# Layer 0's queries and keys: from TensorE transposes to VectorE block transposes and a scratch in DRAM

## The chip, the cores and the metric

The kernel runs on one core of a Trainium2 chip. The metric is the device time of one execution in microseconds (us). A measurement of this kernel can tell about 0.2% (4.2 us) from no change. The core has five engines that matter here: TensorE (PE in the profile), VectorE (DVE), ScalarE (ACT), GpSimd (POOL) and SyncE (SP), which issues nearly all of the transfers. Each works through its own instructions in order and waits on semaphores for the others. Weights come from DRAM (HBM) by 16 DMA engines.

## The reference, cut to what matters

Two decoder layers over 256 tokens of width 2048, float32. Layer 0 mixes tokens with block-sparse attention (16 heads of 128; with 256 tokens there is one block, so it is causal attention), layer 1 with latent attention; each is followed by a gated MLP of width 5632. For layer 0:

```python
h = rms_norm(x, attn_norm[0])
q = rope(rms_norm((h @ wq).reshape(B, S, H, dh), gq), pos, rot)   # H = 16, dh = 128, rot = 32
k = rope(rms_norm((h @ wk).reshape(B, S, H, dh), gk), pos, rot)
v = (h @ wv).reshape(B, S, H, dh)
s = einsum('bqhd,bhkd->bhqk', q, k) * dh ** -0.5                   # causal mask, softmax, times v
y = o.reshape(B, S, H * dh) @ wo
```

A product of queries and keys sums over the head's 128 features. TensorE sums over partitions, so queries and keys have to lie with features on partitions, while `h @ wq` and its norm leave them with tokens on partitions. Something has to turn them.

## The kernel before, in words

All products with weights are done in three parts, for accuracy: a float32 weight piece of 128x512 (`raw`) is split into a rounded part (`whi`, cast by ScalarE, L125) and the rest (`wlo`, subtracted by VectorE, L126), activations likewise, and high x high, high x low and low x high are added up in PSUM.

The work is a list of **quanta**, one for each weight piece. In layer 0 a quantum is six matmuls 128x512 (`tok_major`, L262). The 16 heads are handled in four groups of four heads. A group is 48 quanta: 16 for its queries, 16 for its keys, 16 for its values. I number a group's quanta 0 to 47 below; 48 is then the next group's quantum 0. A step f that was put down by `at(q, f)` is written into the program right behind quantum q's matmuls (what was put down by `first_in` stands ahead of it), and this fixes each engine's order. `ws.split` at quantum q casts the piece of quantum q + 3; five buffers of parts let ScalarE and VectorE run up to about two quanta ahead of TensorE. Loads of 1 MB (four pieces, L90) are issued by SP in the same order, each once VectorE is done with the load three before it.

For a group's queries or keys the class `Heads` has these steps, each a method: `evac` (ScalarE, PSUM to SBUF tile `qk`, times the token's norm, L405), `squares` (VectorE, sums of squares, L410), `rstd` (VectorE, then GpSimd's power, L434), `scaled` (VectorE, four instructions of 128x128 for each half of the tokens, L447), `rotate` (VectorE, four small ones, L472 to L478), and `turned` (L487: TensorE transposes of 128x128 against the identity, into PSUM). `queries_out` and `keys_out` then copy from PSUM to the tiles that the scores use: a rounded part and a float32 copy by ScalarE (L630), the rest by VectorE (L637).

`Head.plan(q, q_values)` puts down a head's scores (TensorE) and mask (VectorE) at q, exponentials at q + 1, normalization at q + 2, the turn of the probabilities at q + 6 and the product with the values at `q_values`. In groups 1 to 3 the queries' `evac` stands at quantum 15, the keys' at 31, the values' (`evac_parts`) at 47. In group 0 the queries' stands at 30 and the keys' at 40, since the norm has to be summed first.

Of the kernel before, what the change touches and what calls it, by code (L numbers as in the profile page):

```python
# [17 lines left out]
P = 128  # L18
# [118 lines left out]
def trunk(ctx: ExitStack, tc: tile.TileContext, a, out):  # L137
# [6 lines left out]
    ps_acc = ctx.enter_context(tc.tile_pool(name="ps_acc", bufs=4, space=PSUM))  # L144
    ps_tp = ctx.enter_context(tc.tile_pool(name="ps_tp", bufs=2, space=PSUM))
    ps_sc = ctx.enter_context(tc.tile_pool(name="ps_sc", bufs=2, space=PSUM))
    ctx.enter_context(tc.manual_schedule())

    mm = nc.tensor.matmul
# [231 lines left out]
        nc.sync.dma_start(out[:, j, :], xT[:, j, :])  # L381


    class Heads:


# [65 lines left out]
        def rotate(self, t, stages=range(4)):  # L452
            if not self.rot:
                return
            n, rot = self.n, self.rot
            hf = rot // 2
            tb, C, Sn = self.tabs
            ct = tb[:, C + t * rot : C + (t + 1) * rot]
            st = tb[:, Sn + t * rot : Sn + (t + 1) * rot]
            x = self.x[:, t]  # L460
            def over(s):
                return s[:, None, :].to_broadcast([P, n, s.shape[1]])

            def part(name):
                r = att_pool.tile([P, 16 * 32], F32, name=name, bufs=2)
                return r[:, : n * rot].rearrange("p (n r) -> p n r", n=n)

            if 0 in stages:
                self.rot_parts = part("ro1"), part("ro2")
            t1, t2 = self.rot_parts  # L470
            if 0 in stages:
                nc.vector.tensor_tensor(t1, x[:, :, :rot], over(ct), op=ALU.mult)  # L472
            if 1 in stages:
                nc.vector.tensor_tensor(t2[:, :, :hf], x[:, :, hf:rot], over(st[:, :hf]), op=ALU.mult)
            if 2 in stages:
                nc.vector.tensor_tensor(t2[:, :, hf:], x[:, :, :hf], over(st[:, hf:]), op=ALU.mult)
            if 3 in stages:
                nc.vector.tensor_tensor(x[:, :, :rot], t1, t2, op=ALU.add)  # L478

        def turned(self, dst, pair, i0):  # L480

# [170 lines left out]
    def keys_out(dst, tp, i0, gain=None):  # L652
# [5 lines left out]
        copied(k0[i0 // 2], src[:, :, :P], gain)  # L658
        rest_of(lo, src, hi, gain)

    def evac_parts(state, key, scale):
        v0, v1 = env[key]
        hi, lo = v0[:, 0], v0[:, 1]
        first_, second = (state["acc"][t][:, :512] for t in range(NT))
        if scale is None:
            nc.scalar.copy(hi, first_)
            nc.vector.tensor_tensor(lo, first_, hi.bitcast(F32), op=ALU.subtract)
            nc.scalar.copy(v1, second)
            return
        r = scale()  # L670
        nc.scalar.activation(hi, first_, AF.Copy, scale=r[:, 0:1])
        nc.vector.scalar_tensor_tensor(
            lo, first_, r[:, 0:1], hi.bitcast(F32), op0=ALU.mult, op1=ALU.subtract
        )
        nc.scalar.activation(v1, second, AF.Copy, scale=r[:, 1:2])

    def plan_heads(q, hs, key, out):

        at(q, hs.evac)
        for t in range(NT):  # L680
            at(q + 1 + t, hs.squares, t)
        at(q + 3, hs.rstd)
        for t in range(NT):
            at(q + 6 + 2 * t, hs.scaled, t)
            at(q + 7 + 2 * t, hs.rotate, t)
        for i0 in (0, 2):
            pair = {}
            q1 = q + 11
            at(q1, lambda hs=hs, p=pair, i0=i0: hs.turned(None, p, i0))
            at(q1, lambda p=pair, i0=i0, key=key: out(env[key], p["tp"], i0))  # L690

    at(-1, n1.scaled, 0)
    def signed_gains():
# [11 lines left out]
    for g in range(4):  # L705
        for kind in "qkv":
            state = {"first": g == 0 and kind == "q"}
            for kt in range(KD):
                q = add(tok_major, state, lambda: n1.h, kt, KD - 1)
                if g == 0 and kind == "q" and kt + 1 < KD:  # L710
                    first(q + 1, n1.scaled, kt + 1)
                if g == 0 and kind == "k" and kt < 12:
                    for j in range(kt * 4 // 3, (kt + 1) * 4 // 3):
                        at(q, n1.square, j)
                        at(q + 1, n1.total, j)
            if g == 0 and kind == "q":
                at(q + 14, n1.sums)
            if kind == "q":
                at(q, moba_tiles, g)
            if kind == "v":  # L720
                at(q, evac_parts, state, ("v", g), lambda: n1.rstd)
                q_v = q
            else:
                hs = Heads(state, 4, P, G_Q if kind == "q" else G_K, 32, (tab, T_MC, T_MS), lambda: n1.rstd)
                plan_heads(q + (0 if g else 15 if kind == "q" else 9), hs, ("qT" if kind == "q" else "kT", g),
                           queries_out if kind == "q" else keys_out)
                q_k = q
        for i in range(4):
            hd = Head(
# [2 lines left out]
            )  # L732
            if g < 3:

                q0 = q_k + (14 if g else 22) + i // 2 * 6
                hd.plan(q0, q0 + 12)
            else:
                q0 = q_k + 14 + 2 * i
                hd.plan(q0, max(q0 + 8, q_v + 3 + i))


# [578 lines left out]
```

## Time and profile before

| what | value |
|---|---|
| median of 3 runs | 2083.99 us (2083.98 to 2084.32) |
| span of the profiled execution | 2081.8 us |
| TensorE clock granted | 1.000 |
| VectorE, ScalarE busy | 68%, 55% of the span |
| DMA | 391.82 MB, mean 188 GB/s |
| layer 0's transposes of queries and keys (L487) | 64, starting between 64.6 and 287.0 us |

The profiled execution gives a span of 2081.8 us, from its first instruction to its last; the runs' times include some 2.2 us around it. In a timeline row the first number is the start in us from the span's start, the second how long the row's instructions took from the first's start to the last's end; then engine, line, operation, tiles, shape and count, and in brackets the engine's idle time before it and what ended it. Consecutive instructions overlap a little: an instruction's result is there later than its successor starts, so a row of three instructions of 0.69 us that takes 1.89 us means one every 0.60 us.

### The profile page before, as it was taken

To read this page: it belongs to the slowest core of one execution; us is meant where nothing else is said; L and a number is where in the kernel's file an instruction comes from. 1 tells how busy PE (TensorE), PEld (TensorE's weight loads), DVE (VectorE), ACT (ScalarE), POOL (GpSimd) and SP (SyncE) were. 2 spreads that over 40 slices of the span, in tenths; PEclk is the share of its full clock that TensorE was granted. 3 is DMA by queue.
4 is the path that set the end of the run, shared out by engine and by line. 5 is a ranking of instruction groups with operands and counts; after the bars stand their busy time and mean duration, and the time that the engine had idled before them with its cause. 6 is when DMAs were issued, how large, how long until landed. Compare 5 with 4: busy or idle time off the path is not lost.

```text
span 2081.8 us, 42114 instructions
## 1 busy us (share of the span) xinstructions
PE 2076.9 (100%) x16742; PEld 2011.4 (97%) x16742; DVE 1415.0 (68%) x2915; ACT 1148.0 (55%) x2248; POOL 46.1 (2%) x36
## 2 busy tenths in 40 slices
PE   9999999999999999999999999999999999999999
PEld 7888889999999999999999889999999999999999
DVE  6877676776666766655556898766667666755554
ACT  6555555555555555555455786655555555544443
POOL 0000000000000000000000110000000000000000
PEclk9999999999999999999999999999999999999999
DMA  7445445555555555555554533555555555555553
GB/s 271 174 173 180 166 162 203 183 193 192 200 187 201 186 199 193 193 202 184 201 194 159 203 124 123 195 190 196 190 202 186 200 189 196 196 198 207 198 205 132
DMA packets 59269, 391.82 MB, mean 188 GB/s; under 512 B 6832, under 2 KB 9520, under 8 KB 13248
## 3 DMA queue, kind: packets, MB, share of 16 engines
q1 hardware_dynamic: 58896, 388.83, 51.7%
q8 instruction: 131, 2.15, 0.4%
q14 instruction: 66, 0.54, 0.1%
q10 hardware_dynamic: 144, 0.26, 0.0%
q0 software_dynamic: 32, 0.04, 0.0%
HBM read 387.01 MB, written 2.10 MB: 187 GB/s over the span
## 4 chain that ended last, share of the span: by engine, by line
PE 100%; DMA 0%; issue 0%; ACT 0%; DVE 0%; POOLq 0%
PE acc L288 26%; PE acc L290 26%; PE acc L289 26%; PE acc L262 18%; PE tp L487 1%; PE tp L566 1%; PE sc L495 0%; PE sc L496 0%; PE sc L494 0%; PE sc L584 0%; PE sc L516 0%; DMA par<-in_par 0%; PE sc L532 0%; PE sc L530 0%; PE tp L357 0%; PE sc L527 0%
## 5 line engine op out<-in xcount | busy, mean ns | idle before, releaser
L126 DVE TENSOR_TENSOR wlo<-raw,whi 128x512 fp32r<-128x512 f32 (+1 forms) x1464 | 996.9, 689 | 375.5 <-ACT whi L125 373.6
L125 ACT CAST whi<-raw 128x512 fp32r<-128x512 f32 (+1 forms) x1463 | 871.2, 620 | 466.9 <-PE acc L289 213.1
L288 PE MATMUL acc<-h,whi 128*128 128x256 f32 x2880 | 795.4, 276 | 0.0
L290 PE MATMUL acc<-h,wlo 128*128 128x256 f32 x2880 | 795.0, 276 | 0.0
L289 PE MATMUL acc<-h,whi 128*128 128x256 f32 x2880 | 794.9, 276 | 0.0
L289 PEld LDWEIGHTS acc<-h,whi 128*128 128x128 f32 x2880 | 540.7, 188 | 0.0
L288 PEld LDWEIGHTS acc<-h,whi 128*128 128x128 f32 x2880 | 540.6, 188 | 0.0
L290 PEld LDWEIGHTS acc<-h,wlo 128*128 128x128 f32 x2880 | 540.6, 188 | 0.0
L288 PE MATMUL acc<-a,whi 128*128 128x256 f32 x1408 | 388.6, 276 | 0.0
L290 PE MATMUL acc<-a,wlo 128*128 128x256 f32 x1408 | 388.6, 276 | 0.0
L289 PE MATMUL acc<-a,whi 128*128 128x256 f32 x1408 | 388.6, 276 | 0.0
L262 PE MATMUL acc<-whi,h 128*128 128x512 f32 (+1 forms) x896 | 268.1, 378 | 0.4 <-ACT h L310 0.4
L289 PEld LDWEIGHTS acc<-a,whi 128*128 128x128 f32 x1408 | 264.3, 188 | 0.0
L290 PEld LDWEIGHTS acc<-a,wlo 128*128 128x128 f32 x1408 | 264.3, 188 | 0.0
L288 PEld LDWEIGHTS acc<-a,whi 128*128 128x128 f32 x1408 | 264.3, 188 | 0.0
L262 PEld LDWEIGHTS acc<-whi,h 128*128 128x128 f32 x896 | 164.8, 188 | 30.3 <-ACT h L310 0.9
L262 PE MATMUL acc<-wlo,h 128*128 128x512 f32 (+1 forms) x448 | 168.4, 376 | 0.0
L288 PE MATMUL acc<-oT,whi 128*128 128x256 f32 x512 | 142.7, 279 | 0.0
L290 PE MATMUL acc<-oT,wlo 128*128 128x256 f32 x512 | 141.6, 277 | 0.0
L289 PE MATMUL acc<-oT,whi 128*128 128x256 f32 x512 | 141.5, 276 | 0.0
L808 DVE TENSOR_TENSOR g<-acc,rstd_b 128x256 f32<-128x256 f32 x88 | 37.5, 426 | 126.0 <-PE acc L290 123.1
L815 ACT ACTIVATE c<-g,par 128x256 f32<-128x256 f32 x88 | 53.1, 603 | 108.0 <-DVE g L808 108.0
(190 smaller groups left out, 1633.7 us busy)
## 6 DMA issues: line engine op xcount, KB each, us to landing
raw<-in_ffn_gu SPq DMA_DIRECT2D x176, 1024.0 KB, 4.8
raw<-in_ffn_down SPq DMA_DIRECT2D x88, 1024.0 KB, 4.8
raw<-in_moba_wk SPq DMA_DIRECT2D x16, 1024.0 KB, 4.8
raw<-in_moba_wv SPq DMA_DIRECT2D x16, 1024.0 KB, 4.8
raw<-in_moba_wo SPq DMA_DIRECT2D x16, 1024.0 KB, 4.8
raw<-in_mla_wo SPq DMA_DIRECT2D x16, 1024.0 KB, 4.8
raw<-in_moba_wq SPq DMA_DIRECT2D x12, 1024.0 KB, 4.8
raw<-in_mla_wkv_a SPq DMA_DIRECT2D x8, 576.0 KB, 3.6
```

Source lines behind the costliest of these rows:

```text
L125: self.nc.scalar.copy(hi[:, :n], w)
L126: self.nc.vector.tensor_tensor(lo[:, :n], w, hi[:, :n].bitcast(F32), op=ALU.subtract)
L262: mm(state["acc"][t][:, :n], src[:, kt, c : c + P], (t_lo if part == 1 else t_hi)[:, :n], start=kt == 0 and part == 0, stop=kt == k_last a ...
L288: mm(o, w_hi, src[:, kt, :S], start=first and k == 0, stop=False, skip_group_check=True)
L289: mm(o, w_hi, src[:, kt, S:], start=False, stop=False, skip_group_check=True)
L290: mm(o, w_lo, src[:, kt, :S], start=False, stop=kt == k_last, skip_group_check=True)
L487: nc.tensor.transpose(tp[:, (i * NT + t) * P : (i * NT + t + 1) * P], flat[:, t, c : c + P], ident)
L566: nc.tensor.transpose(tp[:, c * P : (c + 1) * P], self.s[:, c * P : (c + 1) * P], ident)
L808: nc.vector.tensor_tensor(self.g[:, 2:], self.gate["acc"][:, :S], self.norm.rstd_b, op=ALU.mult)
L815: nc.scalar.activation(self.c, self.g[:, 2:], AF.Identity, bias=par[:, cb : cb + 1], scale=self.cw(2))
```

## The change

Queries and keys of layer 0 are no longer turned on TensorE. VectorE transposes 32x32 blocks (`STREAM_TRANSPOSE`, two instructions a tensor, one for each half of the tokens) from `qk` into a tile `blk`. SP writes `blk` to a scratch in DRAM with four transfers, one for each 32 partitions (128 KB each, in runs of 1 KB), and reads it back into `qk` with one transfer (512 KB, 4 KB to a partition), so that block rows land on the partitions of their block column: that completes the transpose. The copies into the scores' tiles now read `qk` in SBUF and not PSUM; for queries there is one of each kind over all four heads where there were two over two heads each.

The schedule moves with it: `scaled` and `rotate` one quantum earlier (5 to 8 after the `evac`, before 6 to 9), the block transposes and the four writes 9 after it, the read back 11 after it, the copies into the scores' tiles 16 after it (before 11, with the transposes). Scores of the heads, and all that follows them, move by four quanta in groups 1 to 3 and by five in group 0.

```diff
+    dram = ctx.enter_context(tc.tile_pool(name="dram", bufs=2, space=bass.MemoryType.DRAM))
+    def cross_out(srcs, b):
+        w = b.shape[1] // P
+        there = dram.tile([4, 32, 4, w * 32], F32, name=f"there{w}")
+        to = b.rearrange("p (j n t c) -> p t n j c", j=4, t=len(srcs), c=32)
+        for t, src in enumerate(srcs):
+            nc.vector.transpose(to[:, t], src.rearrange("p (n j c) -> p n j c", j=4, c=32))
+        for i in range(4):
+            nc.sync.dma_start(
+                there.rearrange("j a i m -> i a j m")[i],
+                b[32 * i : 32 * (i + 1)].rearrange("a (j m) -> a j m", j=4),
+            )
+        return there
+    def cross_in(dst, there):
+        nc.sync.dma_start(dst, there.rearrange("j a i m -> (j a) (i m)"))
...
+        def cross(self):
+            b = att_pool.tile([P, NT * 4 * P], F32, name="blk", bufs=1)
+            self.there = cross_out([self.x[:, t].rearrange("p n d -> p (n d)") for t in range(NT)], b)
+        def crossed(self):
+            cross_in(self.x.rearrange("p t n d -> p (t n d)"), self.there)
...
+    def crossed_queries(dst, hs):
+        q0, q1 = dst
+        src = hs.heads_of().rearrange("p (n t) i c -> p t n i c", t=NT)
+        hi, lo = (q1[:, part].rearrange("p n (i c) -> p n i c", c=32) for part in range(2))
+        nc.scalar.copy(hi, src[:, 1])
+        nc.vector.tensor_tensor(lo, src[:, 1], hi.bitcast(F32), op=ALU.subtract)
+        nc.scalar.copy(q0.rearrange("p n (i c) -> p n i c", c=32), src[:, 0])
...
         for t in range(NT):
-            at(q + 6 + 2 * t, hs.scaled, t)
-            at(q + 7 + 2 * t, hs.rotate, t)
-        for i0 in (0, 2):
-            pair = {}
-            q1 = q + 11
-            at(q1, lambda hs=hs, p=pair, i0=i0: hs.turned(None, p, i0))
-            at(q1, lambda p=pair, i0=i0, key=key: out(env[key], p["tp"], i0))
+            at(q + 5 + 2 * t, hs.scaled, t)
+            at(q + 6 + 2 * t, hs.rotate, t)
+        at(q + 9, hs.cross)
+        at(q + 11, hs.crossed)
+        at(q + 16, lambda: out(env[key], hs))
...
-                q0 = q_k + (14 if g else 22) + i // 2 * 6
+                q0 = q_k + (18 if g else 27) + i // 2 * 6
...
-                q0 = q_k + 14 + 2 * i
+                q0 = q_k + 18 + 2 * i
```

`crossed_keys` does for the keys, two heads at a time, what `crossed_queries` does for the queries. The scratch pool has two buffers. The temporaries of `rotate` are made as small as they are used.

What this does to the order of the engines is shown at the third group of heads (group 2). SP there (`raw` are loads of weights, `there` is the scratch), first the queries' transfers, then the keys':

```order
 L90 DMA raw<-in_moba_wk 128x2048 x4
-L90 DMA raw<-in_moba_wv 128x2048 x4
-L90 DMA raw<-in_moba_wq 128x2048 x4
+L90 DMA raw<-in_moba_wv 128x2048
+L393 DMA there_2084<-blk 32x4x256 x4
+L90 DMA raw<-in_moba_wv 128x2048
+L400 DMA qk<-there_2084 128x1024
+L90 DMA raw<-in_moba_wv 128x2048 x2
+L90 DMA raw<-in_moba_wq 128x2048
+L393 DMA there_2310<-blk 32x4x256 x4
+L90 DMA raw<-in_moba_wq 128x2048
+L400 DMA qk<-there_2310 128x1024
```

A load of 1 MB now stands between the writes of the scratch and the read of it, and the loads behind both stand behind SP's waits for VectorE and for the writes.

VectorE before, from the queries' first `rotate` of group 2 to the rest of the queries (L637):

```order
L126 TENSOR_TENSOR wlo<-raw,whi 128x512
L447 SCALAR_TENSOR_TENSOR qk<-qk,hr,gains 128x128 x4
L126 TENSOR_TENSOR wlo<-raw,whi 128x512
L472 TENSOR_TENSOR ro_2085<-qk,tab 128x128
L474 TENSOR_TENSOR ro_2086<-qk,tab 128x4x16
L476 TENSOR_TENSOR ro_2086<-qk,tab 128x4x16
L478 TENSOR_TENSOR qk<-ro_2085,ro_2086 128x4x32
L126 TENSOR_TENSOR wlo<-raw,whi 128x512 x2
L637 TENSOR_TENSOR q_1946<-tp,q_1946 128x256 x2
L126 TENSOR_TENSOR wlo<-raw,whi 128x512 x6
```

VectorE now, from the last product of probabilities and values of the group before (`oT`, L622, right behind quantum 19) on:

```order
L622 TENSOR_TENSOR oT<-sc,oT 128x256 x2
L126 TENSOR_TENSOR wlo<-raw,whi 128x512
L465 SCALAR_TENSOR_TENSOR qk<-qk,hr,gains 128x128 x4
L126 TENSOR_TENSOR wlo<-raw,whi 128x512
L490 TENSOR_TENSOR ro_2037<-qk,tab 128x128
L492 TENSOR_TENSOR ro_2038<-qk,tab 128x4x16
L494 TENSOR_TENSOR ro_2038<-qk,tab 128x4x16
L496 TENSOR_TENSOR qk<-ro_2037,ro_2038 128x4x32
L126 TENSOR_TENSOR wlo<-raw,whi 128x512
L465 SCALAR_TENSOR_TENSOR qk<-qk,hr,gains 128x128 x4
```

Behind the second `rotate` the transposes and the later subtraction follow:

```order
L496 TENSOR_TENSOR qk<-ro_2067,ro_2068 128x4x32
L126 TENSOR_TENSOR wlo<-raw,whi 128x512
L391 STREAM_TRANSPOSE blk<-qk 128x4x4x32 x2
L126 TENSOR_TENSOR wlo<-raw,whi 128x512 x7
L698 TENSOR_TENSOR q_1924<-qk,q_1924 128x512
L126 TENSOR_TENSOR wlo<-raw,whi 128x512
```

The two block transposes stand between the pieces, and seven pieces later VectorE comes to an instruction that waits for the read back; the same later place holds two on ScalarE. ScalarE before, from the queries of group 2 to its keys:

```order
L125 CAST whi<-raw 128x512 x11
L630 CAST q_1946<-tp 128x256
L630 COPY q_1945<-tp 128x256
L630 CAST q_1946<-tp 128x256
L630 COPY q_1945<-tp 128x256
L125 CAST whi<-raw 128x512 x5
L405 ACTIVATE qk<-acc,rstd 128x512 x2
L125 CAST whi<-raw 128x512 x11
```

ScalarE now, from the same point to the values:

```order
L697 CAST q_1924<-qk 128x512
L699 COPY q_1923<-qk 128x512
L423 ACTIVATE qk<-acc,rstd 128x512 x2
L125 CAST whi<-raw 128x512 x16
L707 CAST k<-qk 128x512
L709 COPY k_1925<-qk 128x256
L707 CAST k<-qk 128x512
L709 COPY k_1925<-qk 128x256
L721 ACTIVATE v<-acc,rstd 128x512
L725 ACTIVATE v_1928<-acc,rstd 128x512
```

The queries' copies now stand right ahead of the keys' `evac` (quantum 31), and the keys' copies right ahead of the values' (quantum 47), with no cast between. On TensorE the eight transposes of each tensor are gone, 64 in all, and nothing takes their place.

More of the change, by code (lines that the diff above doesn't have):

```diff
@@ L464, in part @@
             def part(name):
-                r = att_pool.tile([P, 16 * 32], F32, name=name, bufs=2)
-                return r[:, : n * rot].rearrange("p (n r) -> p n r", n=n)
+                r = att_pool.tile([P, n * rot], F32, name=name, bufs=2)
+                return r.rearrange("p (n r) -> p n r", n=n)
             if 0 in stages:
@@ L478, in rotate, with heads_of @@
                 nc.vector.tensor_tensor(x[:, :, :rot], t1, t2, op=ALU.add)
+        def cross(self):
[3 more added lines that the diff above has]
+            cross_in(self.x.rearrange("p t n d -> p (t n d)"), self.there)
+        def heads_of(self):
+            x = self.x.rearrange("p t n d -> p (t n d)")
+            return x.rearrange("p (i m c) -> p m i c", i=4, c=32)
         def turned(self, dst, pair, i0):
@@ L659, in keys_out, with crossed_keys @@
         rest_of(lo, src, hi, gain)
+    def crossed_queries(dst, hs):
[5 more added lines that the diff above has]
+        nc.scalar.copy(q0.rearrange("p n (i c) -> p n i c", c=32), src[:, 0])
+    def crossed_keys(dst, hs):
+        k0, k = dst
+        for b in range(2):
+            src = hs.heads_of()[:, 4 * b : 4 * b + 4]
+            hi, lo = (k[b][:, part].rearrange("p n (t i c) -> p (n t) i c", t=NT, c=32) for part in range(2))
+            nc.scalar.copy(hi, src)
+            nc.vector.tensor_tensor(lo, src, hi.bitcast(F32), op=ALU.subtract)
+            nc.scalar.copy(k0[b].rearrange("p n (i c) -> p n i c", c=32), src[:, 0::2])
     def evac_parts(state, key, scale):
@@ L725, in trunk @@
                 plan_heads(q + (0 if g else 15 if kind == "q" else 9), hs, ("qT" if kind == "q" else "kT", g),
-                           queries_out if kind == "q" else keys_out)
+                           crossed_queries if kind == "q" else crossed_keys)
                 q_k = q
```

## The prediction, made before the result was known

> **What bounds the kernel now.** I read the page's busy times and its chain of work first, then the line that the change removes, then TensorE's own timeline around it.
>
> ```profile
> span 2081.8 us, 42114 instructions
> ...
> PE 2076.9 (100%) x16742; PEld 2011.4 (97%) x16742; DVE 1415.0 (68%) x2915; ACT 1148.0 (55%) x2248; POOL 46.1 (2%) x36
> ...
> DMA  7445445555555555555554533555555555555553
> ...
> PE 100%; DMA 0%; issue 0%; ACT 0%; DVE 0%; POOLq 0%
> ```
>
> TensorE never rests, and the whole chain is TensorE. So every moment taken from its order shortens the kernel, as long as whatever feeds it stays in time; and every wait put in its way lengthens it by the same amount. This is the removed line, within the first 400 us:
>
> ```profile
> L487 PE MATMUL tp<-ident,qk x64: 270/272/273, 64.6 to 287.0; 128*128 128x128 f32 x64
> ...
>   ACT k L630: 10.2, 4
> ```
>
> 64 transposes of 272 ns would be 17 us, but matmuls overlap. What they cost is read from starts:
>
> ```profile
> 64.11 0.39 PE L262 MATMUL acc<-wlo,h 128*128 128x512 f32 x1
> 64.34 0.40 PE L262 MATMUL acc<-whi,h 128*128 128x512 f32 x1
> 64.57 1.04 PE L487 MATMUL tp<-ident,qk 128*128 128x128 f32 x8
> 65.36 0.47 PE L262 MATMUL acc<-whi,h 128*128 128x512 f32 x1
> 65.67 0.39 PE L262 MATMUL acc<-wlo,h 128*128 128x512 f32 x1
> ```
>
> The stream starts a matmul every 0.23 us. Eight transposes put the next one off from 64.57 to 65.36, 0.79 us, and the one after starts 0.31 behind it, 0.08 late. A tensor's transposes cost 0.87 us of the stream.
>
> **The gain.** Eight tensors (queries and keys of four groups) by 0.87 us are 7.0 us. Nothing on TensorE replaces them.
>
> **What must stay in time: the pieces.** A quantum takes 1.36 us, as ScalarE's casts show, which wait for TensorE to give a buffer back:
>
> ```profile
> 108.16 0.62 ACT L125 CAST whi<-raw 128x512 fp32r<-128x512 f32 x1 [0.74 <-PE acc L262]
> 109.52 0.62 ACT L125 CAST whi<-raw 128x512 fp32r<-128x512 f32 x1 [0.74 <-PE acc L262]
> ...
> 124.54 1.37 ACT L405 ACTIVATE qk<-acc,rstd 128x512 f32<-128x512 f32 x2 [1.42 <-PE acc L262]
> 125.81 1.65 ACT L125 CAST whi<-raw 128x512 fp32r<-128x512 f32 x3
> ```
>
> The change makes ScalarE wait for the read back, at the copies at quantum 16 after the `evac`. Behind that wait stand the next tensor's `evac` (1.27 us, from 124.54 to 125.81) and all casts, so TensorE's pieces run out after some quanta. VectorE's `lo` waits there too, and SP's read back waits for the writes with loads of weights behind it. I call L the time from the end of VectorE's transposes to the landing of the read back, and ask how much of it each tensor can bear.
>
> **L.** No row shows these transfers; the nearest are a load of 1 MB, the final stores (128 KB in runs of 1 KB, as each write of the scratch), SP's issues, and the rate of DMA while one load and a small one of 176 KB behind it run:
>
> ```profile
> raw<-in_moba_wv SPq DMA_DIRECT2D x16, 1024.0 KB, 4.8
> out<-xT SPq DMA_DIRECT2D x16, 128.0 KB, 1.8
> ```
>
> ```profile
> 95.75 0.33 SPq L90 DMA_DIRECT2D raw<-in_moba_wk  x1
> 96.13 0.42 SPq L206 DMA_DIRECT2D par<-in_par  x1
> ```
>
> ```profile
> 96.00:97.00 1.00, 1.00 (x6) 0.85 (x5) 0.00 (x0) 1.00 (x4) 0.00 (x0) 1.00 0.19 49
> 97.00:98.00 1.00, 1.00 (x6) 0.80 (x6) 0.95 (x3) 1.00 (x2) 0.00 (x0) 1.00 0.80 221
> 98.00:99.00 1.00, 1.00 (x6) 0.84 (x5) 0.96 (x6) 0.20 (x2) 0.00 (x0) 1.00 0.99 410
> 99.00:100.00 1.00, 1.00 (x7) 0.81 (x6) 1.00 (x3) 1.00 (x2) 0.00 (x0) 1.00 0.94 393
> ```
>
> Data flow some 1.2 us after the issue, at 410 GB/s. Four writes are issued from 0.1 us on, one every 0.42: the last at 1.4. The load behind them (SP's order: it stands ahead of the read back in seven of the eight tensors) is issued at 1.8 and lands 4.8 later, at 6.6, if the writes' 0.5 MB (1.3 us at 410) are through when its data start at 3.0. The writes have landed at 1.4 + 1.8 = 3.2, and the read back is issued; its data queue behind the load's and take 1.3 us more: L = 7.9. At half the rate the writes flow from 1.3 to 3.9, push the load by 0.9, and L = 8.8. Were each write to wait for the one before (1.8 each), L would be near 12; with no queueing the read back would still need the writes' 3.2 and about 3.5 of its own, 6.7. I take 8.35, half way between the two inner values, which are nearest to rows of the same size.
>
> [...]
>
> **What the queries can bear.** In groups 2 and 3 the previous group's last values now stand at quantum 19, ahead of both halves' rotations. The same passage one group earlier, at quantum 23:
>
> ```profile
> 112.04 0.28 PE L494 MATMUL sc<-pT,v 128*128 128x256 f32 x1
> 113.11 0.48 PE L262 MATMUL acc<-whi,h 128*128 128x512 f32 x1
> 113.80 0.42 DVE L591 TENSOR_TENSOR oT<-sc,oT 128x256 fp32r<-128x256 f32 x1 [0.16 <-ACT oT L590]
> 114.14 1.13 DVE L447 SCALAR_TENSOR_TENSOR qk<-qk,hr,gains 128x128 f32<-128x128 f32 x4
> 115.19 0.68 DVE L126 TENSOR_TENSOR wlo<-raw,whi 128x512 fp32r<-128x512 f32 x1
> 115.79 0.29 DVE L472 TENSOR_TENSOR ro<-qk,tab 128x128 f32<-128x128 f32 x1
> 116.59 1.28 DVE L126 TENSOR_TENSOR wlo<-raw,whi 128x512 fp32r<-128x512 f32 x2
> 106.60 1.89 DVE L126 TENSOR_TENSOR wlo<-raw,whi 128x512 fp32r<-128x512 f32 x3
> ```
>
> Z is the end of quantum 19 (112.04 there). TensorE resumes 1.07 later, so quantum 31 ends at Z + 17.4 and quantum 34 at Z + 21.5. VectorE is free at Z + 2.1. Then come five rests of pieces of 0.60, two `scaled` of 1.05 and two `rotate` of 0.80: Z + 8.8. The two block transposes are not in the trace. Each handles 512 elements a partition; the nearest rows do that in 0.60 (a subtraction) and, as four instructions, in 1.05 (`scaled`). I take 0.60, since they too are single instructions: done at Z + 10.0, the read back lands at Z + 10.0 + L. ScalarE then copies twice (1.1, at the spacing of casts), does the `evac` (1.27), casts piece 35 (0.62), VectorE subtracts (0.69): 3.7 us, wanted some 0.2 us into quantum 35, at Z + 21.7. L may be 8.0 (0.1 off for semaphores: 7.9). Group 1's queries meet values and turns at quantum 22:
>
> ```profile
> 102.03 0.28 PE L494 MATMUL sc<-pT,v 128*128 128x256 f32 x1
> 105.08 0.28 DVE L410 CUSTOM_DVE_ANT_0 junk<-qk 128x128 f32<-128x128 f32 x1
> ```
>
> VectorE loses 3.05 us there, but TensorE has more to do meanwhile (1.7 us, and 1.07 at quantum 28): the same sum gives L up to 8.25. Group 0's have no heads beside them: 8.5.
>
> **What the keys can bear.**
>
> ```profile
> 82.70 0.38 PE L516 MATMUL sc<-k,q 128*128 128x128 f32 x2
> ...
> 83.86 0.40 PE L262 MATMUL acc<-whi,h 128*128 128x512 f32 x1
> ...
> 132.26 1.14 DVE L447 SCALAR_TENSOR_TENSOR qk<-qk,hr,gains 128x128 f32<-128x128 f32 x4 [0.25 <-POOL hr L434]
> 137.76 1.29 DVE L126 TENSOR_TENSOR wlo<-raw,whi 128x512 fp32r<-128x512 f32 x2
> 139.99 1.04 PE L487 MATMUL tp<-ident,qk 128*128 128x128 f32 x8
> 140.62 0.59 ACT L630 CAST k<-tp 128x512 fp32r<-128x512 f32 x1 [2.54 <-PE tp L487]
> 142.11 2.32 ACT L125 CAST whi<-raw 128x512 fp32r<-128x512 f32 x4
> ```
>
> `scaled` already waits for GpSimd's power, so putting it a quantum earlier moves nothing: rotations end at 137.8 as before, transposes at 139.6. Quantum 42 ends at 140.0, quantum 49 (the scores) at 149.5. The first two heads need one rounded and one float32 copy, 1.0 us: the read back may land at 148.5, L 8.9. ScalarE's line is tighter: copies 1.5 (140.62 to 142.11), the values' two 1.3, a cast and its rest 1.4, wanted in quantum 51, at 152.2 (the scores of two heads, shown at 82.70, take 1.2): it may land at 148.0, L 8.5 at most. Group 0's keys have no load ahead of the read back, so a shorter L: no loss.
>
> **The sum.** At L = 8.35 the queries lose 0.45 in each of groups 2 and 3 and 0.1 in group 1, the keys nothing: 1.0 us. After such a gap VectorE has squares between the pieces (1.46 us a quantum against 1.36), some 0.4 us more in all. 7.0 - 1.4 = 5.6 us less. The profiled execution's 2081.8 would become 2076.2; the median of the runs stands 2.2 above its span, so **2078.4 us** against 2083.99. VectorE's other cost (16 x 0.60 us) and the additional 8 MB lie beside TensorE's work: VectorE's pieces still come 0.5 us or more ahead of their quantum, and a load has about 6 us between landing (4.8) and use (eight quanta, 10.9), of which SP's waits take up to 3. If either cover went, each late piece would show on TensorE in full.
>
> **Rivals.**
> - All is hidden: L below 7.9, as when reads overtake or land sooner. The whole 7.0: 2077.0 us. For it: DMA is idle half of the time here (fourth to seventh digit of its row on the page, tenths in 40 slices). Against: the load ahead in SP's order.
> - Half-rate writes, L = 8.8: queries lose 0.9 twice and 0.55, three groups' keys 0.3 each, group 0's 0.3, and 0.6 behind: 4.2; 2081.2 us. [...]
> - The read back is late: slower than before. The place is ScalarE's wait at quanta 31 and 47; all tensors pay each us of L. Seven of them lose 2 x (L - 7.9) + (L - 8.25) + 4 x (L - 8.5); that passes 7.0 at L = 9.3, with the follow-up at 9.2. Transposes of 1.05 us and half-rate writes make it act as 9.7: 2087 or 2088. Writes one by one, L = 12: some 26 us lost, 2103. For it: no cover is left beyond 1 us. Against: it needs two of the dear ends together.
> - The transposes gave TensorE nothing: no change, 2084. The gap in starts speaks against it.
>
> **Chances.** Forecast 0.35, hidden 0.18, half-rate 0.2, late 0.22, no change 0.05. 0.2% (4.2 us) is about what can be told from no change. The forecast is faster but for 0.04, hidden is all faster, half-rate 0.08 faster and 0.12 same, late 0.04 same: faster 0.57, same 0.25, slower 0.18. The range leaves out the serial writes and the last of the late cases: 2076.3 (0.7 below all hidden, for starts misread by a tenth) to 2088.
>
> **What would show it.** Steps right: no L487 in the first 400 us, TensorE's stream starting every 0.23 us across those places; block transposes near 0.60 us apart; writes landing in 2 to 4 us, the read back about 8 after the transposes; small waits of TensorE for ScalarE's or VectorE's pieces three to four quanta behind each tensor's copies, larger at the queries of groups 2 and 3. Wrong: such waits of over 1 us at every tensor (L above 9), scores waiting for `k`, or casts waiting for loads.

## The result, and the profile after

The changed kernel takes 2099.49 us (median of four executions, 2099.02 to 2100.59) against 2083.98 for the kernel before: a ratio of 1.0075, 95% interval 1.0061 to 1.0089. It is slower by 15.5 us, where 5.6 less was forecast; the prediction's range was 2076.3 to 2088.0. Its profiled execution spans 2096.9 us, 15.1 more than before.

The page of the changed kernel: span, busy times, and the chain that ended last by engine and by line.

```profile
span 2096.9 us, 42070 instructions
...
PE 2080.8 (99%) x16678; PEld 2005.9 (96%) x16678; DVE 1423.5 (68%) x2927; ACT 1147.9 (55%) x2240; POOL 46.1 (2%) x36
...
PE 91%; DMA 3%; DVE 3%; ACT 1%; issue 1%; SPq 0%; POOL 0%; ACTq 0%; DVEq 0%; POOLq 0%
PE acc L289 26%; PE acc L291 26%; PE acc L290 26%; PE acc L263 10%; DMA qk<-there 2%; DMA there<-blk 1%; DVE wlo L126 1%; DVE qk L465 1%; PE tp L597 1%; DVE blk L391 0%; SPq L393 0%; PE tp L518 0%; PE sc L526 0%; PE sc L547 0%; PE sc L527 0%
```

The 64 matmuls are gone (16742 before, 16678 now), but the chain, all TensorE before, leaves it for 9% of the span, and the first lines behind TensorE's own are the two transfers of the scratch. (The 9% are no measure of the loss: while the chain runs through a transfer, TensorE may still be at work: from 204 to 206.75 us, inside the read back shown below, it was busy throughout.) Next, what TensorE waits for in the first 330 us, and what ScalarE waits for between 60 and 310 (us in total, times, longest):

```profile
PE sc L547 <- ACT k L709: 5.2, 4, 1.8
PE acc L263 <- ACT whi L125: 2.6, 3, 1.5
PE acc L263 <- DVE wlo L126: 2.2, 6, 0.7
```

```profile
ACT k L707 <- DMA qk<-there: 20.5, 4, 5.6
...
ACT q L697 <- DMA qk<-there: 17.0, 4, 4.8
```

ScalarE stands still for the read back at all eight tensors, 37.5 us together; 10.0 of it come through to TensorE, which had none of these waits before. Scores wait for the keys (four times), and behind the queries the pieces wait for ScalarE's casts and VectorE's subtractions. One tensor, the queries of group 2, in the chain of work from 195 to 212 us (start, us, what):

```profile
195.36 1.31 DVE blk L391 x2
196.67 0.02 issue
196.69 0.33 SPq L393
...
198.02 3.02 DMA there<-blk
201.03 0.02 issue
201.05 5.70 DMA qk<-there
...
207.30 0.62 ACT q L699
207.91 1.17 ACT qk L423 x2
209.08 0.51 ACT whi L125
209.59 0.03 issue
209.62 0.70 DVE wlo L126
```

L, from the end of the transposes (196.67) to the landing (206.75), is 10.1 us here: 4.4 until the writes have landed and 5.7 for the read. Behind it come the queries' copies, the keys' `evac`, then the first cast, as the prediction's third rival ("the read back is late") had it. Read in the same way, L is 9.4, 8.7, 10.1 and 9.4 for the queries of groups 0 to 3, and 9.0, 9.65, 9.8 and 8.9 for the keys: 9.4 in the mean, against the 8.35 taken.

Setting the starts of the same pieces of both traces side by side gives what each tensor cost: queries 2.35, 1.1, 3.9, 1.8 us, keys 2.1, 4.4, 2.75, 3.1. That is 21.5 us lost. Each tensor's missing transposes gave 0.90 us, 7.2 together. (The other 0.7 of the 15.1 us stand ahead of the first tensor and behind TensorE's last matmul.) The waits listed above hold less than half of the 21.5 us, since a wait is counted from a matmul's modelled end, 0.39 us after its start, while matmuls start every 0.23; short delays do not show in them at all.

**A clock that drops.** Of the 21.5 us, 3.4 are no wait. TensorE around the scores of group 1, and the granted clock (the number behind POOL's) in stretches of 4 us:

```profile
155.22 0.49 PE L547 MATMUL sc<-k,q 128*128 128x128 f32 x2 [1.79 <-ACT k L709]
...
156.72 0.63 PE L263 MATMUL acc<-whi,h 128*128 128x512 f32 x1
157.14 0.63 PE L263 MATMUL acc<-wlo,h 128*128 128x512 f32 x1
157.57 1.05 PE L263 MATMUL acc<-whi,h 128*128 128x512 f32 x2
...
160.44 0.39 PE L263 MATMUL acc<-wlo,h 128*128 128x512 f32 x1
160.67 0.63 PE L263 MATMUL acc<-whi,h 128*128 128x512 f32 x2
```

```profile
156.00:160.00 4.00, 4.00 (x16) 3.28 (x15) 3.47 (x11) 3.12 (x8) 0.00 (x0) 0.57 0.14 27
...
208.00:212.00 4.00, 2.27 (x7) 1.55 (x7) 2.50 (x14) 3.66 (x7) 0.00 (x0) 0.87 0.16 29
212.00:216.00 4.00, 4.00 (x14) 3.10 (x14) 3.08 (x13) 1.24 (x2) 1.95 (x1) 0.70 0.70 262
```

After a wait of 1.79 us matmuls start 0.43 apart instead of 0.23, for 3.4 us, though nothing is waited for. The same follows the wait of 1.51 us that ends at 209.64. The missing parts of the clock (0.43, 0.13 and 0.30 of 4 us each) are 3.4 us.

### The profile page after: what moved, and what is told of

Read it like the earlier page. It is cut to its first block, busy times and chain, and to the rows that moved or that the text cites. A ratio compares the mean times of both kernels' runs of the same rounds, so it can differ in the third digit from the quotient of the medians.

```text
span 2096.9 us, 42070 instructions
## 1 busy us (share of the span) xinstructions
PE 2080.8 (99%) x16678; PEld 2005.9 (96%) x16678; DVE 1423.5 (68%) x2927; ACT 1147.9 (55%) x2240; POOL 46.1 (2%) x36
## 4 chain that ended last, share of the span: by engine, by line
PE 91%; DMA 3%; DVE 3%; ACT 1%; issue 1%; SPq 0%; POOL 0%; ACTq 0%; DVEq 0%; POOLq 0%
PE acc L289 26%; PE acc L291 26%; PE acc L290 26%; PE acc L263 10%; DMA qk<-there 2%; DMA there<-blk 1%; DVE wlo L126 1%; DVE qk L465 1%; PE tp L597 1%; DVE blk L391 0%; SPq L393 0%; PE tp L518 0%; PE sc L526 0%; PE sc L547 0%; PE sc L527 0%
## 5 line engine op out<-in xcount | busy, mean ns | idle before, releaser
L856 DVE TENSOR_TENSOR g<-acc,rstd_b 128x256 f32<-128x256 f32 x88 | 37.5, 426 | 126.0 <-PE acc L291 123.1
```

The lines of the kernel that those rows point to most:

```text
L856: nc.vector.tensor_tensor(self.g[:, 2:], self.gate["acc"][:, :S], self.norm.rstd_b, op=ALU.mult)
```

## The experiments

In the expectations, theory A is that the read back lands too late for what stands behind it on ScalarE. A1 takes the tensors as separate, A2 says that a late tensor makes the next one late too, since the `evac` of the next stands behind the copies of the last. Rival C is that loads, pushed behind SP's waits, starve the casts. Each diff is against the changed kernel unless it says otherwise; ratios are to the kernel before, with their 95% intervals.

**1. Read first.** The read back stands directly behind the writes, ahead of the load of 1 MB.

```diff
-        at(q + 11, hs.crossed)
+        at(q + 9, hs.crossed)
```

> One line differs from the changed kernel: SP issues the read back directly behind the four writes (9 quanta after the evac, not 11), so that no load of 1 MB stands between them; the load now waits for the writes too. In the changed kernel the time from the end of the block transposes to the landing of the read back (L) was 8.7 to 10.1 us. Theory A (the loss is late landing, and of L about 1.5 us is the load ahead of the read): L falls to the 3.2 us that the one read without a load took plus some 4.4 for the writes, 7.6 to 7.9, at or below what the tensors can bear by the prediction's sums; TensorE's waits nearly vanish: 2077 to 2080. Rival B (what costs is the new schedule, ScalarE's and VectorE's work bunched at quanta 31 and 47, or VectorE's additional work): little changes, 2095 to 2100. Rival C (the load, now issued about 3 us later, comes too late): waits move to casts that wait for loads, 2085 to 2095.

2085.2 us, ratio 1.0005 (0.9996 to 1.0015): 14.3 us of the loss are gone, though not all that theory A expected (2077 to 2080). The read back now lands 3.3 us after its issue (median; 4.9 in the changed kernel), and L is 7.0 to 7.4, but 8.7 at group 0's keys, where no load stood between in either kernel. So the load ahead of the read made some 2.2 us of L. Part of what is left is rival C's: ScalarE waits for a load that was pushed back, and behind this wait TensorE's pieces of group 3 come 1.5 us late in all:

```profile
225.10 1.15 ACT L125 CAST whi<-raw 128x512 fp32r<-128x512 f32 x2 [1.42 <-DMA raw<-in_moba_wq]
```

Against the 7.2 us of the missing transposes, the profiled execution still loses 6.7. Besides these 1.5, group 0's scores wait 0.9 us for the keys; the rest are smaller delays that are not taken apart.

**2. Three quanta later.** The copies stand 19 quanta behind the `evac`, and the scores move with them.

```diff
-        at(q + 16, lambda: out(env[key], hs))
+        at(q + 19, lambda: out(env[key], hs))
...
-                q0 = q_k + (18 if g else 27) + i // 2 * 6
+                q0 = q_k + (21 if g else 30) + i // 2 * 6
...
-                q0 = q_k + 18 + 2 * i
+                q0 = q_k + 21 + 2 * i
```

> The changed kernel with the copies and all heads' steps three quanta (4.1 us) later; transfers unchanged. Theory A (late landing alone): L stays 8.7 to 10.1 and each tensor can now bear 12 or more; no TensorE wait on the copies is left and the whole saving of 64 transposes shows: 2077 (2076 to 2078). Rival B (schedule, VectorE's or ScalarE's load): waits stay in part, above 2085. If the saving itself is misread (transposes cost nothing), it ends near 2084 with no waits.

2078.2 us, ratio 0.9972 (0.9961 to 0.9983). L is as before (the read back takes 4.8 us in the median), and TensorE's waits in the first 400 us, apart from one at the kernel's start that all kernels have, come to 0.4 us. So the saving is real, and lateness ate it.

**3. The schedule alone.** The new places, but TensorE's transposes, at quantum 16.

```diff
-        at(q + 9, hs.cross)
-        at(q + 11, hs.crossed)
-        at(q + 16, lambda: out(env[key], hs))
+        for i0 in (0, 2):
+            pair = {}
+            at(q + 16, lambda hs=hs, p=pair, i0=i0: hs.turned(None, p, i0))
+            at(q + 16, lambda p=pair, i0=i0, key=key: out(env[key], p["tp"], i0))
...
-                           crossed_queries if kind == "q" else crossed_keys)
+                           queries_out if kind == "q" else keys_out)
```

> The changed kernel's schedule with TensorE's transposes put back: scaled and rotate a quantum earlier, copies 16 quanta after the evac (transposes just ahead of them), heads four or five quanta later; no block transposes, no scratch, no transfers. Theory A: the schedule costs nothing by itself, 2084 (2083 to 2086). Rival B: the bunching of copies and evac at quanta 31 and 47 costs, 2088 to 2099.

2084.04 us, ratio 1.0 (0.9991 to 1.001). The later scores cost nothing that this can tell (about 2 us).

**4. The crossing unused.** The kernel before, with the block transposes and the transfers added, the read back into a tile that nothing uses. The diff, cut, is against the kernel before.

```diff
+        at(q + 10, hs.cross)
...
+        at(q + 12, hs.crossed)
```

> The kernel before, with its schedule and its TensorE transposes, and beside them the block transposes, the four writes and the read back (10 and 12 quanta after the evac), the last into a tile that nobody reads. Theory A: 8 MB more of transfers and 16 instructions more on VectorE lie beside TensorE's work: 2084 to 2086. Rival D (contention: the transfers delay the loads, or VectorE's pieces come late): 2090 or more, with TensorE waiting for pieces. L can be read here too, without anyone waiting: 8.5 to 10 if it is set by the transfers, below 8 if the waiting kernels themselves made it long.

2084.37 us, ratio 1.0001 (0.9992 to 1.0011). VectorE's 16 instructions and the 8 MB cost nothing when nobody waits for them. L is 9.3 us at group 0's queries, the only tensor here with a load between writes and read, and 7.3 to 8.8 at the others, where 8.5 to 10 was expected if the transfers alone set it: the place of the loads sets it too.

**5. The `evac` first.** The next tensor's `evac` stands ahead of its quantum's other steps, so also ahead of the copies.

```diff
-        at(q, hs.evac)
+        first_in(q, 1, hs.evac)
```

> The changed kernel with one order changed: the evac of each tensor is put ahead of the copies that stand at the same quantum (at 31 the keys' evac before the queries' copies; ScalarE had them the other way round). Theory A2 (late landings hand on: the queries' copies, which wait for their read back, hold the keys' evac, so the keys' whole chain of steps starts late and its read back lands late in turn): the keys' squares start some 1.2 us sooner after the queries' landing, and piece 35 is cast 1.3 us sooner, so that three groups' keys and queries each wait about 1.2 us less, and the two drops of TensorE's clock (some 1.7 us each) go or shrink: 2087 to 2093. Theory A1 (each tensor is late by its own transfers alone, nothing is handed on): only the queries' pieces gain, 2095 to 2098.

2095.47 us, ratio 1.0055 (1.004 to 1.007): 4.0 us better than the changed kernel, between the two expectations. What TensorE waits for between 60 and 330 us:

```profile
PE sc L547 <- ACT k L709: 5.9, 4, 1.9
PE acc L263 <- DVE wlo L126: 1.5, 3, 0.7
PE acc L263 <- ACT whi L125: 0.6, 1, 0.6
```

The gain is at the queries: those of groups 1 to 3 cost 0.7 us in all, where they cost 5.1 without the clock in the changed kernel (the waits for `wlo` and `whi` are group 0's, but for 0.3). The keys gain nothing. The scores wait for `k` four times, 5.9 us together where it was 5.2, and the clock drops twice here too, behind two of these waits (mean clock 0.998, as in the changed kernel). The keys' `evac` does end sooner, but their next step, the squares (L428), stands on VectorE behind the queries' subtraction (L698), which waits for the same read back, and behind a piece:

```profile
129.56 0.69 DVE L698 TENSOR_TENSOR q<-qk,q 128x512 fp32r<-128x512 f32 x1 [3.34 <-ACT q L697]
130.60 0.69 DVE L126 TENSOR_TENSOR wlo<-raw,whi 128x512 fp32r<-128x512 f32 x1 [0.35 <-ACT whi L125]
131.21 0.29 DVE L428 CUSTOM_DVE_ANT_0 junk<-qk 128x128 f32<-128x128 f32 x1
```

So in group 1 they start 11.3 us before quantum 43 begins on TensorE, as in the changed kernel; in the kernel before it was 12.9, up to the transposes that stand there.

**6. The keys alone.** TensorE turns the queries, at quantum 16; only the keys go through the scratch.

```diff
+        if key[0] == "qT":
+            for i0 in (0, 2):
+                pair = {}
+                at(q + 16, lambda hs=hs, p=pair, i0=i0: hs.turned(None, p, i0))
+                at(q + 16, lambda p=pair, i0=i0, key=key: out(env[key], p["tp"], i0))
+            return
...
-                           crossed_queries if kind == "q" else crossed_keys)
+                           queries_out if kind == "q" else crossed_keys)
```

> The changed kernel with only the keys through the scratch; the queries are turned by TensorE at quantum 16 after their evac, as in the run of the schedule alone. Half of the saving is left, 3.5 us. The transfers of the keys are as in the changed kernel (L about 9 to 10). Theory A1 (the keys' own L against the 8.5 that the prediction let them bear): three groups lose about 1 us each, 2083 to 2085. Theory A2, with the queries' copies ahead of the keys' evac even when nothing waits (1.1 us): the keys can bear some 7 and lose 2 to 3 us in each of three groups, 2086 to 2090; less than the changed kernel's, whose queries land late as well.

2090.93 us, ratio 1.0036 (1.0022 to 1.0049). Half of the saving (3.5 us) is left, so the keys lose 10.4 us by themselves, somewhat more than either theory gave them, with L from 8.5 to 10.0. Group 1 in this kernel, ScalarE, VectorE, ScalarE, TensorE:

```profile
124.61 0.37 ACT L661 CAST q<-tp 128x256 fp32r<-128x256 f32 x1 [2.56 <-PE tp L518]
...
125.66 1.30 ACT L423 ACTIVATE qk<-acc,rstd 128x512 f32<-128x512 f32 x2
```

```profile
139.42 1.30 DVE L391 STREAM_TRANSPOSE blk<-qk 128x512 f32<-128x512 f32 x2
```

```profile
149.98 0.62 ACT L707 CAST k<-qk 128x512 fp32r<-128x512 f32 x1 [5.19 <-DMA qk<-there]
150.50 0.40 ACT L709 COPY k<-qk 128x256 f32<-128x256 f32 x1
```

```profile
150.96 0.49 PE L547 MATMUL sc<-k,q 128*128 128x128 f32 x2 [1.39 <-ACT k L709]
```

The queries' copies at quantum 31 put the keys' `evac` at 125.66, where the kernel before had it at 124.54. The transposes end at 140.72 and not at the 139.6 of the prediction, while TensorE is ready for the scores at 149.57. With 1.0 us for the copies the read back had to land by 148.6, 7.9 after the transposes; it took 9.2. In the other groups L less TensorE's wait is 7.9 too, and in the changed kernel it is 7.9, 7.9, 8.6 and 7.9.

**7. All ports.** Each of the four writes takes a quarter of the columns of all 128 partitions instead of 32 partitions in full. (Block rows are then not exchanged, so scores come from wrong features; the amount of work is the same.)

```diff
-                there.rearrange("j a i m -> i a j m")[i],
-                b[32 * i : 32 * (i + 1)].rearrange("a (j m) -> a j m", j=4),
+                there.rearrange("j a i m -> (j a) i m")[:, i],
+                b[:, i * w * 32 : (i + 1) * w * 32],
```

> Of the changed kernel, only what each of the four writes covers differs: all 128 partitions and a quarter of the columns, and not 32 partitions and all columns; 128 KB in runs of 1 KB to the same places' spacing in the scratch, and the same read back. The block rows are then not exchanged, so attention is computed from wrongly turned queries and keys; the amount of work is the same. Theory P (a write from 32 partitions moves at about half the rate): the last write lands 1.8 to 2.1 us after its issue and not 2.9 to 3.1, L falls by 0.9 or so and the time to 2089 to 2094. Rival Q (what makes the writes slow is their number, or DRAM): landing times and the total stay, 2098 to 2100.

2098.61 us, ratio 1.0072 (1.0055 to 1.0088): not to be told from the changed kernel. The rates while the writes flow (last number, GB/s; the share of the DMA engines ahead of it), first of the changed kernel, then of this one:

```profile
197.50:198.00 0.50, 0.50 (x4) 0.38 (x4) 0.50 (x2) 0.41 (x1) 0.00 (x0) 1.00 0.88 188
198.00:198.50 0.50, 0.50 (x4) 0.42 (x3) 0.50 (x2) 0.00 (x0) 0.00 (x0) 1.00 0.92 201
```

```profile
196.50:197.00 0.50, 0.50 (x4) 0.42 (x3) 0.50 (x2) 0.00 (x0) 0.00 (x0) 1.00 0.81 268
197.00:197.50 0.50, 0.50 (x4) 0.42 (x3) 0.48 (x1) 0.41 (x1) 0.00 (x0) 1.00 0.81 266
```

The writes from 32 partitions moved at some 190 GB/s, about half of the 400 of the loads (393 and 410 in the prediction's rows); those from 128 partitions at 267, with shorter time to landing (median 2.0 us; 2.5 in the changed kernel). (267 need not be the most that 128 partitions allow: one write of 128 KB is issued every 0.45 us, which is 290 GB/s.) But the read back took 5.6 instead of 4.9, and L stayed between 8.8 and 9.8: what the writes gained, the read spent behind the load. So theory P was right that the writes would gain (the rate from 32 partitions is 0.7 of the other and not half), and rival Q on the time.

**8. One quantum later.** As 2, by one quantum instead of three.

```diff
-        at(q + 16, lambda: out(env[key], hs))
+        at(q + 17, lambda: out(env[key], hs))
...
-                q0 = q_k + (18 if g else 27) + i // 2 * 6
+                q0 = q_k + (19 if g else 28) + i // 2 * 6
...
-                q0 = q_k + 18 + 2 * i
+                q0 = q_k + 19 + 2 * i
```

> The changed kernel with the copies and the heads' steps one quantum (1.36 us) later. At three quanta later everything was hidden (2078.2). Theory A2: each tensor gets 1.36 us, the waits of TensorE that were 0.8 to 1.8 us mostly go or shrink, no wait is left that is long enough for a drop of the clock, and less is handed on from queries to keys: 2083 to 2088. If lateness were not handed on and the clock did not drop: eight tensors by up to 1.36 us less, 2089 to 2091.

2083.98 us (ten executions, 2082.46 to 2086.27), ratio 1.0 (0.9991 to 1.0009). This is within theory A2's expectation. 1.36 us more time for each tensor give back 15.5 us: eight times 1.36 are 10.9, and the profiled execution has no drop of the clock (mean 1.000), which cost the changed kernel's 3.4. The two waits for `k` that remain come to 1.7 us.

**9. The queries alone.** The mirror of 6: TensorE turns the keys.

```diff
+        if key[0] == "kT":
+            for i0 in (0, 2):
+                pair = {}
+                at(q + 16, lambda hs=hs, p=pair, i0=i0: hs.turned(None, p, i0))
+                at(q + 16, lambda p=pair, i0=i0, key=key: out(env[key], p["tp"], i0))
+            return
...
-                           crossed_queries if kind == "q" else crossed_keys)
+                           crossed_queries if kind == "q" else keys_out)
```

> Only the queries go through the scratch; the keys are turned by TensorE again, at quantum 16 behind their evac, with the new schedule. 3.5 us are saved (4 tensors by 0.87). Theory (each tensor is late for itself, and a late one of the queries also makes the keys behind it late, since the keys' evac stands behind the queries' copies on ScalarE): the queries lose here what they lost in the changed kernel at their own quanta, 2.35 + 0.8 + 2 to 3.9 + 1.5, some 6.7 to 8.6 us, so 2087 to 2089 us, 3 to 5 us slower than before. With the keys alone 6.9 slower, the two then add up to 10 to 12, and the 15.5 of the two together hold 4 to 6 us that one hands on to the other. Rival (the losses are separate): 8.6 slower than before, 2092.6 us, since 15.5 less 6.9 is 8.6. Waits of TensorE behind the queries only, for ScalarE's and VectorE's pieces, none for k.

2088.17 us, ratio 1.0025 (1.0015 to 1.0035): the queries lose 7.7 us, within the expectation. With 10.4 of the keys that is 18.1 against the 22.5 of both (15.5 + 7.0), so 4.4 us belong to neither alone. I had expected to find there what one tensor hands on to the next. But the changed kernel's profiled execution lost 3.4 by its clock, and this kernel shows by itself what the clock does: six of its nine executions took 2087.8 to 2088.6 at a mean clock of 1.000, three 2090.2 to 2092.2 at 0.999. Against that, one execution of the changed kernel took 2099.65 at a clock of 1.000. By the times, handing on is thus worth between nothing and 4 us. The traces show 1.3 us of it: in groups 1 and 3 of the changed kernel, whose keys' steps start late behind the queries, pieces come 0.2 us late up to quantum 43 and 0.4 us up to quantum 45, where the keys-alone kernel loses less than 0.1. At the scores nothing is handed on, since TensorE is late by then as well: the keys bear 7.9 us there in both kernels (experiment 6).

**10. Two quanta later.** The scores at 20, 29 and 20 likewise.

```diff
-        at(q + 16, lambda: out(env[key], hs))
+        at(q + 18, lambda: out(env[key], hs))
...
```

> The changed kernel with the copies two quanta later (18 behind the evac) and the scores with them. With none later the time was 2099.5, with one 2084.0, with three 2078.2. Theory (a wait of the transfer's latency L that was measured at 8.7 to 10.1 us against what the tensors could bear, 7.7 to 8.5 us, and that grows by one quantum, 1.36 us, for each quantum of delay): now 10.4 to 11.2 can be borne, so only the two tensors with L near 10 may still show tenths of a us: 2078 to 2080. Rival (the gain of three later comes from something else that goes with the later scores, and grows evenly): 2081 us, half way between one and three, with waits of TensorE left at several tensors.

2078.23 us, ratio 0.9974 (0.9963 to 0.9984): as good as three later. ScalarE's waits for the read back have shrunk from 37.5 to 9.0 us, and TensorE's for what hangs on it are gone:

```profile
ACT q L697 <- DMA qk<-there: 4.7, 4, 2.1
...
ACT k L707 <- DMA qk<-there: 4.3, 4, 2.1
```

The rival's even gain (2081 us) is out: the time falls by 15.5, 5.7 and 0.0 us from one quantum to the next, as it must when a wait runs out.

**11. Read first and one quantum later.** 1 and 8 together.

```diff
-        at(q + 11, hs.crossed)
-        at(q + 16, lambda: out(env[key], hs))
+        at(q + 9, hs.crossed)
+        at(q + 17, lambda: out(env[key], hs))
...
```

> The read back stands directly behind the writes, ahead of the load of 1 MB (L then was 7.0 to 7.4 us, except 8.8 at the group 0 keys, which have their load ahead anyway), and the copies come one quantum later than in the changed kernel (17 behind the evac). Theory (latency against what can be borne): with read first alone 2085.2 and one later alone 2084.0; both together bear 9.1 to 9.8 against L of 7.0 to 8.8, so nothing waits for the crossing, and what is left is the load that the reads push back (casts waiting up to 1.4 us for a load): 2077.5 to 2081 us. If the late load is what kept read first from gaining, the time stays above 2082, with casts (L125) waiting for loads. Rival (the time goes by the load's place): 2084 to 2085, as read first alone.

2080.46 us (2078.94 to 2081.04), ratio 0.9982 (0.9972 to 0.9992). Within the expectation, and TensorE waits for nothing behind the crossings, yet it is 2.2 us behind the kernels that copy two or three quanta later. Between 60 and 310 us ScalarE still waited 4.2 us for loads of `raw`, up to 2.1 at once, where the kernel before waited for none; whether these made the 2.2 us isn't shown.

The best kernel here is the changed one with the copies and scores two or three quanta later: 2078.2 us, 5.8 below the kernel before.

## Why the prediction was wrong

**Right: the gain and what hides.** TensorE's stream runs on where the transposes were; each tensor gains 0.90 us (0.87 taken), and two or three quanta later the kernel is 5.8 us faster. What is missing to 7.2 went mostly, at three quanta later, into two pieces of group 1's quanta that come 0.7 and 0.3 us late. The schedule (experiment 3) and VectorE's and the DMA's additional work (4) are free. The block transposes are 0.65 us apart, for 0.60 taken:

```profile
L391 DVE STREAM_TRANSPOSE blk<-qk x16: 668/688/706, 63.6 to 299.5; 128x512 f32<-128x512 f32 x16
```

**Right: what the queries of groups 1 to 3 can bear.** Their first late piece was late by 0.8, 2.2 and 1.5 us with L at 8.7, 10.1 and 9.4: each bore 7.9, for which 8.25, 7.9 and 7.9 were taken. (In the queries-alone kernel it is 7.9 again, with L at 9.1, 10.7 and 9.5.) Behind it came 0.3 us more in groups 1 and 3, as VectorE's squares stood between the pieces (0.4 in all was foreseen), and 1.7 by the clock in group 2.

**Wrong: the term L**, 8.35 for a measured 9.4, above even the upper inner value. The writes' part was 3.2 us and is 4.4. The prediction named half-rate writes and gave them 0.2. The half rate in its 8.8 was the author's assumption, and no run shows it: the changed kernel's writes moved at 190 GB/s, which is 0.7 of the 267 of writes from all 128 partitions (experiment 7), and half fits only the 400 of the loads, which go the other way. The faster writes did not save L: it was 9.2 in the mean (7), where the prediction's sum gave 7.9. The read's place behind the load decides (1), and that load took 5.3 to 6.7 us to land in the changed kernel, for 4.8 taken. Where SP has no load between, at group 0's keys, a load issued 2.6 us ahead of the writes is still landing beside them instead (chain of the changed kernel; the transposes end at 81.99):

```profile
83.36 4.35 DMA there<-blk
...
87.79 3.21 DMA qk<-there
```

The read takes 3.2 us, as nothing is ahead of it, but the writes take 5.7, and L is 9.0; "so a shorter L: no loss" was wrong there. By the prediction's own bounds, the measured L cost 8.4 us: 0.9, 0.45, 2.2 and 1.5 at the queries, 0.5, 1.15, 1.3 and 0.4 at the keys (group 0's taken at the 8.5 of the others).

**Wrong: the bounds of the keys**, 8.5 (by its own figures, 148.0 less 139.6, 8.4). At the scores, for which 8.9 was taken, they bore 7.9, 7.9, 8.6 and 7.9 (experiment 6). The failing sentence is that "rotations end at 137.8 as before, transposes at 139.6". With the keys alone the transposes ended at 140.72: the queries' copies now stand ahead of the keys' `evac`, and even without any wait they put it off by 1.1 us. In the changed kernel the queries' late read back holds the keys' steps as well, on ScalarE and on VectorE, so that taking the `evac` alone out of its way moved nothing (5): the transposes end 1.3 us after quantum 43 begins in groups 1 and 3, where the prediction had them 0.4 before it (0.1 after it in group 2, whose pieces ran at the lower clock meanwhile). The prediction saw this order, and charged it to the queries' pieces, but not to the keys' start.

In all, the keys lost 2.1, 2.7 (4.4 less 1.7 of the clock), 2.75 and 3.1 us, 7.3 more than their L cost by the bounds of the prediction. TensorE's waits for the scores are 5.2 of the 10.65 us; the rest are smaller delays of pieces, of which 1.3 are those up to quanta 43 and 45 (9) and the others are not taken apart. Group 0's queries bore 7.0 rather than 8.5, 1.5 us more; group 1's the 0.35 of above.

**Missing: the clock**, 3.4 us in the profiled execution. 8.4 for L, 9.15 for bounds, 0.6 behind the queries' pieces and 3.4 are the 21.5 lost. (The bounds are here worked out from the losses, so that this adds up is no test. The waits at the scores and experiment 6 test the keys' part; experiments 1, 8 and 10 test that lateness is the cause.)

The rival that came true, the late read back, had a chance of 0.22 and was priced at 2087 or 2088: its formula gives 2 x 1.5 + 1.15 + 4 x 0.9 = 7.8 at L = 9.4, about no change. It fell short by the keys' bounds and the clock.

## What to carry to other kernels

When a step is replaced by one of longer latency, work out its slack with the new order, not the old one: whatever now stands ahead of the next chain's first instruction on the same engine shortens that chain's slack too, and this has to be asked of every engine that the chain passes: to move its first instruction alone gained the keys nothing (experiment 5: waits for `k` of 5.9 us, 5.2 in the changed kernel). With eight such waits in a row, one quantum of 1.36 us more or less decided 15 us, so leave a spare quantum where it is free (here it was: with the later scores alone the time was 2084.04 us, experiment 3). A transfer that somebody waits for is put ahead of the bulk load in its queue, or given the time that the load takes: put first, the read back landed 3.3 us after its issue and not 4.9 (experiment 1). Making the writes faster, 267 GB/s instead of 190, gave nothing (2098.61 us, experiment 7).

## What the runs showed of the hardware

Waits of 1.5 to 2.1 us on TensorE were at times followed by 3.41 us at a granted clock of 0.50 (0.43 us from start to start instead of 0.23): after 1.79 and 1.51 us in the changed kernel, after 1.89 and 1.93 with the `evac` first, and in the queries-alone kernel after 2.07:

```profile
207.15 0.50 PE L263 MATMUL acc<-whi,h 128*128 128x512 f32 x1 [2.07 <-ACT whi L125]
```

In the keys-alone kernel a wait of 2.12 us at 301.76 had no such sequel, nor had one of 1.94 in experiment 7 (mean clock 1.000 in both). So the length of the wait alone does not tell them apart. In the changed kernel's records of the clock the two slow stretches begin at 156.36 and at 210.97, 54.61 us apart, which is 16 times the 3.413 that each lasts. Here are, of the changed kernel, the 3.41 us ahead of the first stretch, the stretch itself and the 3.41 us ahead of the second; then those ahead of the stretch in the queries-alone kernel; then, of the keys-alone kernel, 6.8 us around the end of its wait (TensorE's busy time stands behind the comma, the clock behind POOL's):

```profile
152.96:156.38 3.42, 1.62 (x12) 1.19 (x11) 1.35 (x2) 2.13 (x5) 0.00 (x0) 1.00 0.65 270
156.38:159.78 3.40, 3.40 (x11) 2.72 (x11) 2.87 (x9) 2.52 (x6) 0.00 (x0) 0.50 0.12 19
207.58:210.99 3.41, 1.68 (x7) 0.85 (x6) 1.91 (x9) 3.41 (x7) 0.00 (x0) 1.00 0.03 14
```

```profile
204.41:207.82 3.41, 1.17 (x4) 0.39 (x3) 1.39 (x3) 3.41 (x7) 0.00 (x0) 1.00 0.04 17
```

```profile
300.05:303.46 3.41, 1.70 (x14) 1.69 (x15) 1.69 (x3) 2.67 (x6) 0.00 (x0) 1.00 0.31 131
303.46:306.88 3.42, 3.00 (x24) 2.60 (x23) 2.90 (x8) 2.54 (x7) 0.00 (x0) 1.00 0.23 41
```

Ahead of these three slow stretches TensorE was busy 1.62, 1.68 and 1.17 us of 3.41. With the changed kernel's trace laid off in steps of 3.413 us from its two starts, TensorE was busy 2.2 us or more in every other step from 10 us on up to its last matmul. What decides whether a wait has such a sequel is not shown: these are three stretches, and no run moved a wait to test it.
